# Routing of two tiles at once, and the last layer's experts in order of their token counts

## The chip, the core and the metric

The program runs on one core of one Trainium2 chip. The metric is the device time of one execution in microseconds (us); of several runs the median counts. The engines are PE (matrix multiplication; PEld is its weight load), DVE (VectorE), ACT (ScalarE), POOL (GpSimd) and SP (SyncE, which here issues the DMAs of the weights). The kernel leaves the order within each engine's queue to a planner that simulates a timeline when the program is built; `issue_after` holds instructions of a block behind a given one.

## What is computed

Two layers of a transformer over 256 latent and 256 context tokens with 1024 features. Each layer is a mixer followed by a mixture of experts. What matters here is the second part:

```python
def grouped_moe(h, router_w, router_b, w1, w3, w2):
    ...
    scores = jax.nn.softmax((t @ router_w).astype(jnp.float32), axis=-1)
    sel = scores + router_b.astype(jnp.float32)
    gscore = jnp.sum(lax.top_k(sel.reshape(-1, N_GROUPS, EXPERTS_PER_GROUP), TOP_K)[0], axis=-1)
    best = jnp.argmax(gscore, axis=-1)
    ...
    _, idx = lax.top_k(jnp.where(in_grp, sel, -jnp.inf), TOP_K)
    ...
    for e in range(N_EXPERTS):
        a = jax.nn.silu(t @ w1[e]) * (t @ w3[e])
        y = y + gate[:, e:e + 1] * (a @ w2[e])
    return y.reshape(shape)
```

There are 16 experts in 4 groups, and each token goes to 2 of them. Layer 0 routes 512 tokens (4 tiles of 128), the last layer only the 256 latent tokens (2 tiles), which are 512 assignments. The weights of one expert are six units of 1 MiB: w1 and w3 in four, w2 in two. All values are fp32; matmuls run in fp32 or as split parts in fp32r.

## The kernel before

**Norm and routing.** The last part of the mixer takes the tiles one by one: it adds the residual (L955), squares (L959), transposes (`norm2_turn`, L1102), and multiplies with the router weights (`norm2_logits`, L1115 to L1127). `norm2_rows` makes the normalized rows h2 (L1142, L1144; some halves go through ACT and POOL, L1139 and L1140). `route_tile` turns the logits of one tile into two one-hot choices O and their sum r_ind (L1288) by a chain of small DVE instructions on 16 columns, and into gate weights. `route_slots` counts on PE how many earlier tokens chose the same expert (`earlier`, L1318) and gives each token its slot: r_sg (L1305) in the last layer, one-hots r_oh (L1328) in layer 0. There `dispatch` then makes the index lists, a branch follows for overflowing experts (L1836), and the rows of the first expert are gathered by an indirect DMA. Three buffers for gathered rows are zeroed by POOL (L1458).

**The last layer's experts** (`experts_blocks`). The 16 experts go one after the other in their natural order, 64 slots each. `group` gathers the tokens of four experts by matmuls with one-hots goh (L1583, L1572). The loop at the end of the function goes over the experts: `act` (silu L1631, gate L1635) for e, the branch, the first half of `inner` for e+1 (L1618), `turn` (L1641, L1643) and `outer` for e (L1618 on aT), then the second half of `inner` for e+1. Every second expert the rows of a pair are split in two parts (`parts`, L1698, L1699) and added to the residual in PSUM (`combine`, L1690). The residual itself is put there by eight matmuls with the identity (L1728) at the start of the function.

An expert with more than 64 tokens needs a second pass, `extra`, over the same weights. It stands in a branch for every expert:

```python
            with tc.If(v > B):
                extra(e)
```

The count v is loaded into a register on PE, ACT and DVE; all three go through the branch.

**Weights.** `weights` gives the units in the order of their use, and `prefetch` issues their loads on SP into a ring of 11 units of 1 MiB. A load waits until PE has used what lay in its buffer.

## Time and profile before

| | us |
|---|---|
| median of 3 runs | 1284.99 (1282.62 to 1285.81) |
| profiled execution | 1283.58 |
| its span in the profile | 1281.8 |
| PE busy | 1182.5 (92%) |
| DVE busy | 733.4 (57%) |
| ACT busy | 585.9 (46%) |
| POOL busy | 222.8 (17%) |

The busy times are means over stages that differ: the span has two mixers, two routings and two expert stages. A matmul group of `xN` lists its instructions; an fp32 matmul is two of them. "ACTq" or "PEq" as what ended a wait is the engine's queue itself, here its branch, not an instruction that computes. [...]

### The profile page before, as it was taken

The page shows a single profiled execution, that of the slowest core. Times are in us where ns is not written, and L with a number is a line of the kernel's source. Part 1 is how long each engine was busy: PE and PEld are TensorE (multiplying, and loading weights), DVE is VectorE, ACT ScalarE, POOL GpSimd, SP SyncE. Part 2 cuts the span into 40 slices and gives each one's busy share as a digit, 9 for nine tenths or more (in the row PEclk, how much of TensorE's full clock was granted, in tenths as well). Part 3 has the DMA queues.
Part 4 walks back from the last instruction along what each step waited for, and adds up shares of the span by engine and source line. Part 5 has one row for each costly group of instructions (what it writes and reads, how often), then busy time and mean ns, then how long its engine had stood idle before and what let it go on. Part 6 is the DMA issues. An engine that isn't in the chain of part 4 may idle for free. (4 is left out here: it accounts for less than half of the span.)

```text
span 1281.8 us, 16756 instructions
## 1 busy us (share of the span) xinstructions
PE 1182.5 (92%) x6133; PEld 802.3 (63%) x6133; DVE 733.4 (57%) x1284; ACT 585.9 (46%) x1001; POOL 222.8 (17%) x251
## 2 busy tenths in 40 slices
PE   5899999999987999999999799999997898989885
PEld 3588887546755788887776588986554434334322
DVE  3475454365587999998889957544558222211112
ACT  4374343255333888888776565533443111111011
POOL 2205012022043111111104524003202000000000
PEclk9999999999987999999999999999997999999898
DMA  9524115983437999999976351217966399999951
GB/s 348 217 99 177 66 66 195 352 302 120 149 148 265 362 381 378 380 383 357 354 292 239 117 178 46 99 67 239 369 255 222 145 389 411 418 407 414 379 194 71
DMA packets 55744, 322.05 MB, mean 251 GB/s; under 512 B 9211, under 2 KB 9371, under 8 KB 22360
## 3 DMA queue, kind: packets, MB, share of 16 engines
q1 hardware_dynamic: 48552, 302.77, 61.6%
q0 software_dynamic: 7088, 17.92, 4.4%
q8 instruction: 63, 1.03, 0.3%
q14 instruction: 41, 0.34, 0.1%
HBM read 313.65 MB, written 14.68 MB: 256 GB/s over the span
## 5 line engine op out<-in xcount | busy, mean ns | idle before, releaser
L191 DVE TENSOR_TENSOR wlo<-raw,whi 128x1024 fp32r<-128x1024 f32 x264 | 323.3, 1248 | 81.3 <-ACT whi L190 78.6
L190 ACT CAST whi<-raw 128x1024 fp32r<-128x1024 f32 x264 | 272.6, 1049 | 173.1 <-PE ps L1390 28.6
L1618 PE MATMUL ps<-raw,xT 128*64 128x512 f32 x424 | 111.3, 611 | 19.3 <-ACTq L1743 10.4
L1389 PE MATMUL ps<-whi,xh 128*128 128x512 f32 x256 | 103.0, 403 | 0.7 <-ACT whi L190 0.7
L1391 PE MATMUL ps<-wlo,xh 128*128 128x512 f32 x256 | 99.4, 400 | 4.1 <-DVE wlo L191 4.0
L1390 PE MATMUL ps<-whi,xl 128*128 128x512 f32 x256 | 101.4, 396 | 0.0
L362 PE MATMUL ps<-hl,whi 128*128 128x512 f32 (+1 forms) x256 | 96.5, 378 | 4.8 <-DVE hl L342 4.8
L363 PE MATMUL ps<-hh,wlo 128*128 128x512 f32 (+1 forms) x256 | 94.0, 376 | 4.4 <-DVE wlo L191 4.4
L361 PE MATMUL ps<-hh,whi 128*128 128x512 f32 (+1 forms) x256 | 94.1, 378 | 1.3 <-ACT hh L339 1.2
L1618 PEld LDWEIGHTS ps<-raw,xT 128*64 128x64 f32 x424 | 33.2, 139 | 76.7 <-issue 49.6
L379 PE MATMUL ps<-whi,hh 128*128 128x512 f32 x176 | 71.7, 408 | 0.0
L380 PE MATMUL ps<-whi,hl 128*128 128x512 f32 x176 | 70.0, 398 | 0.0
L381 PE MATMUL ps<-wlo,hh 128*128 128x512 f32 x176 | 68.6, 397 | 0.0
L1635 DVE SCALAR_TENSOR_TENSOR s<-ps,ggate,s 64x512 f32<-64x512 f32 x16 | 12.0, 749 | 92.5 <-ACT s L1631 68.4
L220 PE MATMUL ps<-raw,svec 128*32 128x512 f32 (+1 forms) x416 | 62.1, 606 | 1.9 <-DMA raw<-in_ada_w_dram 1.9
L1654 DVE TENSOR_TENSOR yp<-ps,X 64x512 f32<-64x512 f32 x32 | 22.0, 689 | 70.9 <-PE ps L1618 70.7
L1391 PEld LDWEIGHTS ps<-wlo,xh 128*128 128x128 f32 x256 | 48.0, 188 | 22.1 <-DVE wlo L191 11.4
L362 PEld LDWEIGHTS ps<-hl,whi 128*128 128x128 f32 x256 | 50.5, 197 | 14.1 <-DVE hl L342 5.5
L1618 PE MATMUL ps<-raw,aT 128*64 128x512 f32 x232 | 58.2, 594 | 1.0 <-ACT aT L1643 1.0
L363 PEld LDWEIGHTS ps<-hh,wlo 128*128 128x128 f32 x256 | 49.8, 197 | 12.6 <-DVE wlo L191 4.6
L361 PEld LDWEIGHTS ps<-hh,whi 128*128 128x128 f32 x256 | 49.8, 196 | 10.6 <-ACT hh L339 2.6
L1389 PEld LDWEIGHTS ps<-whi,xh 128*128 128x128 f32 x256 | 48.3, 189 | 11.7 <-ACT whi L190 1.9
(422 smaller groups left out, 2289.1 us busy)
## 6 DMA issues: line engine op xcount, KB each, us to landing
raw<-in_exp_w_dram SPq DMA_DIRECT2D x174, 1024.0 KB, 7.6
raw<-in_ada_w_dram SPq DMA_DIRECT2D x48, 1024.0 KB, 6.9
raw<-in_w_in_dram SPq DMA_DIRECT2D x28, 1024.0 KB, 8.5
raw<-in_w_out_dram SPq DMA_DIRECT2D x8, 1024.0 KB
whi<-in_exp_w_dram SPq DMA_DIRECT2D x16, 512.0 KB, 13.5
wlo<-in_exp_w_dram SPq DMA_DIRECT2D x16, 512.0 KB, 7.7
yd<-oz SPq DMA_DIRECT2D x8, 512.0 KB, 8.8
rpbt<-in_rpb_rows_dram POOLq DMA_DIRECT2D x16, 256.0 KB, 12.3
```

The lines of the kernel that those rows point to most:

```text
L190: self.nc.scalar.copy(hi[:, :n], raw[:, k:k + n])
L191: self.nc.vector.tensor_tensor(lo[:, :n], raw[:, k:k + n], hi[:, :n].bitcast(F32), op=ALU.subtract)
L361: nc.tensor.matmul(o, hi[:, kk, s], self.hh[:, k, tok], start=k == 0, stop=False)
L362: nc.tensor.matmul(o, hi[:, kk, s], self.hl[:, k, tok], start=False, stop=False)
L363: nc.tensor.matmul(o, lo[:, kk, s], self.hh[:, k, tok], start=False, stop=k == KT - 1)
L379: nc.tensor.matmul(acc[g], self.hh[:, k, s], hi[:, kk], start=k == 0, stop=False)
L380: nc.tensor.matmul(acc[g], self.hl[:, k, s], hi[:, kk], start=False, stop=False)
L381: nc.tensor.matmul(acc[g], self.hh[:, k, s], lo[:, kk], start=False, stop=k == KT - 1)
L1389: nc.tensor.matmul(ps, xh, hi[:, kk], start=k == 0, stop=False)
L1390: nc.tensor.matmul(ps, xl, hi[:, kk], start=False, stop=False)
L1391: nc.tensor.matmul(ps, xh, lo[:, kk], start=False, stop=k == KT - 1)
L1618: mm = nc.tensor.matmul(o[c:c + B], x, wt, start=k == 0, stop=k == n - 1, tile_position=(0, c), skip_group_check=True)
```

## The change

`route_tile` becomes `route_tiles`: two tiles go through one chain, with instructions on two tiles' columns wherever no per-token scalar is needed. Layer 0 routes tiles 0 and 1 within the loop over the tiles and tiles 2 and 3 behind it; the last layer routes its two tiles at once behind the last logits. `norm2_rows` loses the form that used ACT and POOL, and the rows of the last two tiles come ahead of the last logits; h2l of the last tile comes behind r_ind (`norm2_parts`). The eight matmuls of the residual move from the start of `experts_blocks` to behind the last logits. The three buffers of layer 0 are zeroed by ACT instead of POOL.

In the last layer `sort` orders the experts 4 to 15 by falling count on DVE, and moves their counts, slots and gates along. Positions 0 to 3 keep their experts. The weights from position 4 on are loaded from an address that SP takes from a register, loaded from `order`. Of 512 assignments at most seven of the sorted twelve can have more than 64, so positions 11 to 15 have no branch. A matmul of the identity into the next accumulator is added before each branch. `extra` transposes its one-hots earlier and uses two PSUM buffers.

```diff
-                    self.route_tile(l, n - 1)
                     self.norm2_rows(l, tiles[n - 1])
+                if n == 2:
+                    self.route_tiles(l, 0)
...
+        self.norm2_rows(l, tiles[-2])
         self.norm2_turn(g, 1)
+        self.norm2_scale(g)
+        self.norm2_rows(l, g, False)
         self.norm2_logits(l, g, 1)
-        self.route_tile(l, n - 1)
-        self.norm2_rows(l, tiles[-2])
-        with self.tc.issue_after(self.scored.ins):
-            for i in range(n):
-                self.route_slots(l, i)
-        self.route_tile(l, n)
-        self.route_slots(l, n)
-        self.norm2_rows(l, tiles[-1])
+        if not l:
+            with self.tc.issue_after(self.scored.ins):
+                self.route_slots(l, 0)
+        if l:
+
+            self.acc = [[self.ps() for _ in range(2)] for _ in tiles]
+            with self.tc.issue_after(self.scored.ins):
+                for i, t in enumerate(tiles):
+                    for h in range(2):
+                        nc.tensor.matmul(self.acc[i][h], self.ident, self.X[:, t, h * 512:(h + 1) * 512], start=True,
+                                         stop=False, skip_group_check=True)
+        self.route_tiles(l, n - 1)
+        self.route_slots(l, n - 1)
+        if l:
+            self.norm2_parts(g)
...
+    def norm2_scale(self, g):
+        q = self.work.tile([P, 4], F32, name="n2q", bufs=4)
+        nc.vector.tensor_scalar(q[:, 0:1], self.ss2[:, 0, g:g + 1], 1.0 / D, EPS, op0=ALU.mult, op1=ALU.add)
+        nc.vector.scalar_tensor_tensor(q[:, 1:2], self.ss2[:, 1, g:g + 1], 1.0 / D, q[:, 0:1], op0=ALU.mult, op1=ALU.add)
+        nc.gpsimd.tensor_tensor(self.r2[:, g:g + 1], q[:, 1:2], self.mhalf[:, 0:1], op=ALU.pow)
+
+    def norm2_rows(self, l, g, parts=True):
...
-            spare = g == 3 and half == 1 or g == 2 and l == 0
-            if spare:
-                nc.scalar.mul(h2[:, s], self.X[:, g, s], self.r2[:, g:g + 1])
-                nc.gpsimd.tensor_tensor(h2[:, s], h2[:, s], self.A2[r][:, s], op=ALU.mult)
-            else:
-                nc.vector.scalar_tensor_tensor(h2[:, s], self.X[:, g, s], self.r2[:, g:g + 1], self.A2[r][:, s],
-                                               op0=ALU.mult, op1=ALU.mult)
-            (nc.vector if half and not spare else nc.gpsimd).tensor_tensor(h2[:, s], h2[:, s], self.S2[r][:, s],
-                                                                           op=ALU.add)
+            nc.vector.scalar_tensor_tensor(h2[:, s], self.X[:, g, s], self.r2[:, g:g + 1], self.A2[r][:, s],
+                                           op0=ALU.mult, op1=ALU.mult)
+            (nc.vector if half or g == 3 else nc.gpsimd).tensor_tensor(h2[:, s], h2[:, s], self.S2[r][:, s], op=ALU.add)
...
+            if parts:
+                self.norm2_parts(g)
         else:
             nc.sync.dma_start(self.hd[i * P:(i + 1) * P], h2)
 
+    def norm2_parts(self, g):
+
+        with self.tc.issue_after(self.chosen.ins) if g == 3 else ExitStack():
+            self.nc.vector.tensor_tensor(self.h2l[:, g - 2], self.h2, self.h2h[:, g - 2].bitcast(F32), op=ALU.subtract)
...
-            for e in range(NE):
+            for p in range(NE):
+                x = p
+                if p >= FIXED:
+                    x = self.nc.values_load(self.order[0:1, p - FIXED:p - FIXED + 1], engines=(ET.SP,), min_val=0,
+                                            max_val=NE - 1)
                 for u in range(6):
-                    yield w[l, e, u]
+                    yield w[l, p, u] if p < FIXED else w[l, ds(x, 1), u].rearrange("o p f -> (o p) f")
...
+    def route_tiles(self, l, i):
...
+        V.tensor_reduce(mx, self.logits[:, w], axis=AX.X, op=ALU.max, negate=True)
+        for j in each:
+            nc.scalar.activation(sc[:, j], self.logits[:, i + j], AF.Exp, bias=mx[:, j:j + 1], accum_out=sm[:, j:j + 1])
         V.reciprocal(rs, sm)
-        V.scalar_tensor_tensor(sel, sc, rs, self.rb, op0=ALU.mult, op1=ALU.add)
...
+        for j in each:
+            V.scalar_tensor_tensor(sel[:, j], sc[:, j], rs[:, j:j + 1], self.rb, op0=ALU.mult, op1=ALU.add)
+
+        s4 = sel.rearrange("p n (g e) -> p (n g) e", g=4)
+        p6 = pr.rearrange("p n g e -> p (n g) e")
+        V.tensor_tensor(p6[:, :, 0:3], s4[:, :, 0:3], s4[:, :, 1:4], op=ALU.add)
...
+        for j in each:
+            V.scalar_tensor_tensor(key[:, j, 0:4], gs[:, j], gm[:, j:j + 1], self.rank16[:, 0:4], op0=ALU.is_equal,
+                                   op1=ALU.mult)
+        V.tensor_reduce(k1, key[:, :, 0:4], axis=AX.X, op=ALU.max)
+        V.tensor_tensor(low, key[:, :, 0:4], wide(k1, 4), op=ALU.is_lt)
+        V.scalar_tensor_tensor(s4, bcast(low.rearrange("p n (g o) -> p (n g) o", o=1), [P, 4 * n, 4]), NEG, s4,
+                               op0=ALU.mult, op1=ALU.add)
+        O = R["O"]
+        for k in range(2):
+            V.tensor_reduce(c0, sel, axis=AX.X, op=ALU.max)
+            for j in each:
+                V.scalar_tensor_tensor(key[:, j], sel[:, j], c0[:, j:j + 1], self.rank16, op0=ALU.is_equal, op1=ALU.mult)
+            V.tensor_reduce(c1, key, axis=AX.X, op=ALU.max)
+            V.tensor_tensor(O[:, w, k], key, wide(c1, NE), op=ALU.is_equal)
+            if k == 0:
+                V.scalar_tensor_tensor(sel, O[:, w, 0], 4 * NEG, sel, op0=ALU.mult, op1=ALU.add)
+        self.chosen = V.tensor_tensor(R["ind"][:, w], O[:, w, 0], O[:, w, 1], op=ALU.add)
...
+        both, wt = t("both", [2, NE]), t("wt", [2])
+        with self.tc.issue_after(self.chosen.ins):
+            for j in each:
+                G.tensor_tensor(both[:, j], O[:, i + j], bcast(sc[:, j, None, :], [P, 2, NE]), op=ALU.mult)
+                nc.scalar.activation(R["gw"][:, i + j], both[:, j], AF.Copy, accum_out=wt[:, j, 0:1])
+            V.reciprocal(wt[:, :, 1], wt[:, :, 0])
+            for j in each:
+                nc.scalar.mul(R["gw"][:, i + j], both[:, j], wt[:, j, 1:2])
+                if l:
+                    G.tensor_tensor(R["gate"][:, i + j], R["gw"][:, i + j, 0], R["gw"][:, i + j, 1], op=ALU.add)
...
+        pp = self.ps()[:, 0:n * NE].rearrange("p (n e) -> p n e", n=n)
+        for j in range(n):
+            self.earlier(i + j, pp[:, j])
+            self.routed = V.scalar_tensor_tensor(R["sg"][:, w], pp, 1.0, R["ind"][:, w], op0=ALU.add, op1=ALU.mult)
...
+            both = self.moeA.tile([P, n, 2, NE], F32, name="rt_both2")
+            for c in range(2):
+                V.tensor_tensor(both[:, :, c], R["O"][:, w, c], pp, op=ALU.mult)
+            V.tensor_reduce(R["slot"][:, w], both, axis=AX.X, op=ALU.add)
+            for j in range(n):
+                self.slotted(i + j)
...
-            nc.gpsimd.memset(x, 0.0)
+            nc.scalar.mul(x.rearrange("p (k s) -> p k s", k=KT), bcast(self.slots[:, None, :], [P, KT, P]), 0.0)
...
+        def sort():
...
+            c = R["cntf"][:, FIXED:]
+            V.scalar_tensor_tensor(key, c, 16.0, self.rank16[:, FIXED:], op0=ALU.mult, op1=ALU.add)
+            V.tensor_tensor(tmp, row(key), col(key), op=ALU.is_gt)
+            V.tensor_reduce(rank, tmp, axis=AX.X, op=ALU.add)
+            V.tensor_tensor(mat, row(rank), col(self.slots[:, 0:NS]), op=ALU.is_equal)
+
+            def moved(dst, src):
+                V.tensor_tensor(tmp, mat, row(src), op=ALU.mult)
+                V.tensor_reduce(dst, tmp, axis=AX.X, op=ALU.add)
+            moved(val, self.rank16[:, FIXED:])
+            V.tensor_scalar(self.order, val, -1.0, 16.0, op0=ALU.mult, op1=ALU.add)
+            moved(val, c)
+            V.tensor_copy(cnts, val)
+            for i in range(nt):
+                moved(sgs[:, i], R["sg"][:, i, FIXED:])
+                moved(gts[:, i], R["gate"][:, i, FIXED:])
...
-            for i in range(nt):
-                for e in range(4):
-                    self.routed = V.tensor_scalar(oh[:, i, :, e], slots1, R["sg"][:, i, 4 * g + e:4 * g + e + 1], None,
-                                                  op0=ALU.is_equal)
+            for b in range(2):
+                for i in range(nt):
+                    V.tensor_tensor(oh[:, i, b], bcast(slots1[:, b, None, :], [P, 4, B]),
+                                    bcast(SG(i, g)[:, :, None], [P, 4, B]), op=ALU.is_equal)
...
-            ps = self.ps()
-            inner(lambda k: x[:, k], W[e], range(KT), ps)
-            aT = turn(*act(ps))
-            ps = self.ps()
...
+            py = self.ps()
+            inner(lambda k: x[:, k], W[e], range(KT), py)
+            aT = turn(*act(py), ps)
...
-        acc = [[self.ps() for _ in halves] for _ in range(nt)]
-        for i in range(nt):
-            for h, s in enumerate(halves):
-                nc.tensor.matmul(acc[i][h], self.ident, X[:, 2 + i, s], start=True, stop=False, skip_group_check=True)
+        acc = self.acc
...
+        sort()
...
+        seven = FIXED + nt * P * 2 // (B + 1)
+
+        def value(e):
+            src = R["cnt"][0:1, 1 + e:2 + e] if e < FIXED else cnts[0:1, e - FIXED:e - FIXED + 1]
+            return nc.values_load(src, engines=(ET.PE, ET.Activation, ET.DVE), min_val=0, max_val=nt * P)
...
-            with tc.If(v > B):
-                extra(e)
+                nc.tensor.matmul(A[e + 1][:, 0:B], self.ident, self.ident[:, 0:B], start=True, stop=True,
+                                 skip_group_check=True)
+            if e < seven:
+                with tc.If(v > B):
+                    extra(e)
             self.prefetch(len(self.raws) - 2)
-            if e + 1 < NE:
+            if e + 1 < seven:
                 v = value(e + 1)
```

## Rows read from the trace of the kernel before

**Rows 1.** Stretches: us; PE, PEld, DVE, ACT, POOL busy (instructions); clock; DMA share; GB/s.
```profile
377.00:403.00 26.00, 14.78 (x95) 9.09 (x96) 21.76 (x101) 8.70 (x24) 11.74 (x16) 0.63 0.82 300
981.00:1002.00 21.00, 13.85 (x73) 8.96 (x73) 16.47 (x74) 5.39 (x16) 9.55 (x15) 0.70 0.27 100
1064.00:1179.00 115.00, 103.53 (x502) 47.69 (x498) 26.18 (x41) 14.25 (x24) 1.31 (x2) 0.99 1.01 412
1190.00:1200.00 10.00, 7.46 (x25) 1.88 (x20) 2.58 (x3) 1.64 (x2) 0.00 (x0) 0.83 1.02 422
1209.00:1234.00 25.00, 21.86 (x96) 10.01 (x94) 3.44 (x5) 1.83 (x4) 0.00 (x0) 0.86 0.70 265
```

**Rows 2.** Timeline of DVE, layer 0 routing: start, length (us), line, output<-input [idle before].
```profile
372.54 0.16 DVE L1263 RECIPROCAL rt_col<-rt_col 128x1 f32<-128x1 f32 x1 [0.47 <-ACT rt_sc L1262]
...
383.09 0.22 DVE L1127 SCALAR_TENSOR_TENSOR logits<-ps,rstd,rbS 128x16 f32<-128x16 f32 x1
...
392.23 0.23 DVE L1284 TENSOR_SCALAR r_o<-rt_key,rt_col 128x16 f32<-128x16 f32 x1
392.50 0.17 DVE L1288 TENSOR_TENSOR r_ind<-r_o 128x16 bf16<-128x16 f32 x1
```

**Rows 3.** Timeline of PE, where the first expert of layer 0 starts.
```profile
402.52 1.73 PE L713 MATMUL ps<-ident,A 128*128 128x128 f32 x7 [5.08 <-PEq L1836]
```

**Rows 4.** Timeline of DVE, routing of the last layer.
```profile
984.26 0.22 DVE L1127 SCALAR_TENSOR_TENSOR logits<-ps,rstd,rbS 128x16 f32<-128x16 f32 x1
...
985.60 1.19 DVE L1277 TENSOR_TENSOR rt_sel<-rt_sel,rt_low 128x16 f32<-128x16 f32 x1
...
994.16 0.18 DVE L1288 TENSOR_TENSOR r_ind<-r_o 128x16 bf16<-128x16 f32 x1
...
1010.71 0.74 DVE L1635 SCALAR_TENSOR_TENSOR s<-ps,ggate,s 64x512 f32<-64x512 f32 x1 [9.32 <-ACT s L1631]
```

**Rows 5.** Timeline of POOL, routing of the last layer.
```profile
984.28 2.48 POOL L1144 TENSOR_TENSOR h<-h,X 128x512 f32<-128x512 f32 x2
```

**Rows 6.** Waits from 1005 us on: who waited <- for whom: us, times, longest.
```profile
PE ps L1618 <- ACTq L1743: 13.8, 9, 2.6
...
PE ps L1618 <- DMA raw<-in_exp_w_dram: 3.9, 4, 1.2
```

**Rows 7.** Timeline of ACT, the last experts: silu (L1631) and the copy ex.
```profile
1179.11 0.59 ACT L1631 ACTIVATE s<-ps 64x512 f32<-64x512 f32 x1 [8.68 <-PE ps L1618]
...
1205.87 0.59 ACT L1631 ACTIVATE s<-ps 64x512 f32<-64x512 f32 x1 [5.21 <-PE ps L1618]
1213.74 0.59 ACT L1664 COPY ex<-ps 128x512 f32<-128x512 f32 x1 [7.28 <-PE ps L1572]
...
1246.08 0.59 ACT L1631 ACTIVATE s<-ps 64x512 f32<-64x512 f32 x1
...
1256.48 0.59 ACT L1631 ACTIVATE s<-ps 64x512 f32<-64x512 f32 x1 [5.20 <-PE ps L1618]
```

**Rows 8.** Timeline of PE, the last experts: where PE stood, and after the extra.
```profile
1179.80 3.65 PE L1618 MATMUL ps<-raw,xT 128*64 128x512 f32 x16 [0.72 <-ACTq L1743]
...
1192.40 1.07 PE L1618 MATMUL ps<-raw,xT 128*64 128x512 f32 x2 [1.54 <-ACTq L1743]
1194.47 5.34 PE L1618 MATMUL ps<-raw,xT 128*64 128x512 f32 x14 [1.00 <-DMA raw<-in_exp_w_dram]
...
1234.16 3.65 PE L1618 MATMUL ps<-raw,xT 128*64 128x512 f32 x16
...
1246.77 3.65 PE L1618 MATMUL ps<-raw,xT 128*64 128x512 f32 x16 [1.54 <-ACTq L1743]
```

**Rows 9.** Groups of instructions by line, 930 us on: count | busy us, mean ns | idle before.
```profile
L1728 PE MATMUL ps<-X,ident 128*128 128x512 f32 x8 | 5.7, 882 | 0.0
...
L1142 DVE SCALAR_TENSOR_TENSOR h<-X,rstd 128x512 f32<-128x512 f32 x3 | 2.2, 749 | 0.9 <-POOL rstd L1122 0.8
```

**Rows 10.** Waits of the queue of SP from 990 us on.
```profile
SPq L182 <- PE ps L1618: 78.6, 10, 18.5
```

More of the change, by code (lines that the diff above doesn't have):

```diff
@@ L37 @@
 NPT = 4
+FIXED = 4
 ET = mybir.EngineType
@@ L1118, in norm2_logits @@
             return
-        q = w.tile([P, 4], F32, name="n2q", bufs=4)
-        nc.vector.tensor_scalar(q[:, 0:1], self.ss2[:, 0, g:g + 1], 1.0 / D, EPS, op0=ALU.mult, op1=ALU.add)
-        nc.vector.scalar_tensor_tensor(q[:, 1:2], self.ss2[:, 1, g:g + 1], 1.0 / D, q[:, 0:1], op0=ALU.mult, op1=ALU.add)
-        nc.gpsimd.tensor_tensor(self.r2[:, g:g + 1], q[:, 1:2], self.mhalf[:, 0:1], op=ALU.pow)
+        if g not in self.scaled:
+            self.norm2_scale(g)
         part = w.tile([P, 512], F32, name="lpart", tag="t2", bufs=T2)[:, :P]
@@ L1289, in route_tile @@
+        self.chosen = V.tensor_tensor(R["ind"][:, w], O[:, w, 0], O[:, w, 1], op=ALU.add)
         if not l:
-            nc.scalar.mul(R["val"][:, i, :, 0], O, self.tokp[:, i:i + 1])
-            nc.scalar.copy(R["val"][:, i, 1, 1], O[:, 1])
+            for j in range(i, i + n):
+                nc.scalar.mul(R["val"][:, j, :, 0], O[:, j], self.tokp[:, j:j + 1])
+                nc.scalar.copy(R["val"][:, j, 1, 1], O[:, j, 1])
         G = nc.gpsimd
-        G.tensor_tensor(both, O, bcast(sc[:, None, :], [P, 2, NE]), op=ALU.mult)
@@ L1315, in earlier @@
+    def earlier(self, i, pp):
         nc, R = self.nc, self.R
[L1316 removed]
         for j in range(i + 1):
[L1318 to L1320 removed]
+            nc.tensor.matmul(pp, self.tri if j == i else self.onesb, R["ind"][:, j], start=j == 0,
+                             stop=j == i, skip_group_check=True)
     def slotted(self, i, rnd=0):
```

96 lines of the change are left out of this document (36 added, 60 removed).

## The prediction

> **What bounds the kernel now.** I read the windows first. They cut out the stretches that the change touches: the routing of the first layer, the routing of the last layer, and the last layer's experts [rows 1]. Between 377 and 403 us PE is busy for 14.8 of 26 us, at a mean granted clock of 0.63, while DVE is busy for 21.8: a chain of small DVE steps stands between the mixer and the first expert. Between 981 and 1002 us it is the same: DVE 16.5 of 21 us, PE 13.9, clock 0.70. In the last layer's experts (1064 to 1179 us) two things run near full: PE is busy for 103.5 of 115 us, and the DMA engines show a share of 1.01 at 412 GB/s.
>
> Then the timelines of the two routings. In layer 0 the last tile's logits start at 383.09 and the last r_ind ends at 392.67, 9.6 us later [rows 2]; the first expert's transposes start at 402.52 [rows 3]. In the last layer the same two points are 984.26 and 994.34, 10.1 us apart [rows 4]. The reader is to see that two tiles' chains take turns there, and that a 16-element step lasts 1.19 us, where others last 0.17 to 0.23, while POOL works on the rows h [rows 2, 4, 5].
>
> Then the waits of the expert stage: before the L1618 matmuls PE stands 13.8 us in 9 waits released by ACT's branch and 3.9 us in 4 waits for weights [rows 6]. Last, the ACT and PE timelines: one silu per expert gives the pace [rows 7]. Only one expert runs `extra`: the only ex copy follows the 14th silu, so it is expert 13. The extra fills the window 1209 to 1234, and the next expert starts at 1234.16 [rows 1, 8]: 25 us. During it the DMA share is 0.70 instead of 1.01.
>
> **The change part by part.** Minus is a gain.
>
> *Layer 0, routing by pairs.* After the last logits one chain of 26 DVE instructions serves two tiles. Six are followed by one that doesn't depend on them; I put 0.1 us on each of those, and 0.22 on each of the other 20, by the dependent steps 392.23 and 392.50, 0.27 apart, whose durations are 0.23 and 0.17 [rows 2]: 5.0 us. The exps come in between: DVE pauses 0.47 us for one [rows 2], so some 0.7 for two. The chain is 5.7 us against 9.6: -3.9. Back come four one-hots instead of two behind the last r_ind and a wider multiplication, some +0.6. The rows of tiles 2 and 3 now take seven half-row steps on DVE, each about 0.7 us by the nearest row [rows 9], 5 us between the last X and its logits; PE and ACT work for the logits meanwhile, but a logits instruction can land behind two of them: 0 to +1.7, I take +0.9. Sum -2.4. Bounds: 0, if it is not the chain but the gather's landing or the branch at L1836 that sets 402.52 [rows 3] and these don't move along, and -4. I take -2.4 since gather and dispatch stand behind r_ind in program order. The three zero fills that go from POOL to ACT are activations of 1024 elements, about 1 us each; ACT is busy for 8.7 of the 26 us [rows 1], so 0.
>
> *Last layer, routing.* The chain is 5.7 against 10.1: -4.4. The rows of the last tile are four DVE steps of about 0.7 us [rows 9] ahead of the logits: 0 to +1.7, taken +0.8. ACT's cast h2h of 1024 elements, about 1 us, may come before the exps: 0 to +1, taken +0.4. POOL no longer works on these rows, so the 1.19 us step and its like [rows 4] should shrink; that is within the -4.4. The residual's eight matmuls (5.7 us, 0.88 each at the low clock [rows 9]) move ahead of r_ind. Their place today puts r_sg some 0.6 us late; against that stands the h2l subtraction, now behind r_ind: 0 together. But PE then idles up to 2 us before the gather, and in this stretch the clock did fall after idling (0.70 on the mean [rows 1]): the gather's 32 instructions of 256 columns are about 3.7 us, by half of the 0.23 us that one of 512 takes (16 in 3.65 [rows 8]), and double at half clock: 0 to +3.7, taken +0.7. Sum -2.5, bounds -4.5 and +1.5.
>
> *Sort.* 18 small DVE instructions of at most 144 elements; 512 elements take 0.75 us and 16 take 0.17 to 0.23 [rows 2, 9], so some 0.3 each, 5 to 6 us. DVE waits 9.32 us at exactly that place, while PE runs the first expert [rows 4]: 0. Without that cover the whole 6 us would stand before the first act.
>
> *Expert order and register addresses.* Expert 13 holds the largest count from the fifth on, so its extra moves from the 14th to the 5th place and still costs 25 us. SP loads twelve registers, each at the head of six weight DMAs. What is queued behind such a load is the weight stream; who waits is PE, but only once the units in flight are used up. The ring holds 11 units of 1 MiB, 6 of them in use, so 5 are in flight: 5 x 2.55 us (1 MiB at 412 GB/s) = 12.7 us of cover. No row shows a register load on SP; nearest is the wait of PE at a branch, 0.72 to 1.54 us at four late experts [rows 8]. I take 0; bounds 0 and 12 x 1.54 = +18.5, which needs the cover to be gone at each one.
>
> *No branch for the last five.* At experts 11, 12 and 14 PE stands 0.72, 1.54 and 1.54 us, released by ACT's branch [rows 8]; I add 0.7 for the 14th place (no row, as the extra ran there) and 0.3 for the last: -4.8. At expert 12 the branch wait and the weight wait of 1.00 that follows it are where the clock fell: 0.83 in 1190 to 1200 us [rows 1], that is a third of the time at half speed, 1.7 us of matmuls: -1.7. Bounds: -8, and 0 if PE waits for the same ACT and DVE work at a semaphore.
>
> [...]
>
> *What is late next: the weights.* In 1064 to 1179 a position's six units take 6 x 2.55 = 15.3 us. The last four steps of silu (expert 11 to 15) took 26.8 (two of them), 40.2 and 10.4 us [rows 7]. Without the extra's 25, the waits named above and the clock, these are 46 us of work. Four positions' weights are 4 x 15.3 = 61.1 us. Five units are ahead when they begin, because the extra at the 5th place lets the ring fill and the experts up to the 11th, with their gathers, are no faster than the weights: 61.1 - 12.7 = 48.4, so 2.4 us of new waits for weights: +2.4. Bounds: 0, and +15 if no lead is left. In the before, the extra itself covered this place. Of the four older weight waits (3.9 us [rows 6]) the one at expert 12 goes, as the ring is fuller: -1.0 (0 to -3.9).
>
> *The added matmul* on the identity before each branch: two instructions of 64 columns, well under the 0.23 us of one with 512 [rows 8], with their weight loads 0.25 us for both. Where a branch follows PE waits anyway; on the rest +1.0 (0 to +3.8 for fifteen).
>
> Sum: -2.4 - 2.5 - 4.8 - 1.7 + 2.4 - 1.0 + 1.0 = -9.0 us. The profiled execution took 1283.58 us, so 1274.6; the median of the runs, 1284.99, lies 1.4 higher, so I predict 1276.
>
> **The rivals.** *More than that.* The weights keep up to the end (no +2.4), both routings give what their chains say (-3.9 and -4.4), the clock stays up: about -15, 1270. For it: 412 GB/s is a mean, and the DMA engines have slack in the extra. Against: a wait for weights, 1.00 us, stood at expert 12 already.
>
> *Waits that only move.* PE meets ACT at a semaphore instead of the branch, or the weights take all of 6.5 back; layer 0's start is set by the gather; what is left is the last layer's routing: -2.5, 1282.5. For it: PE's waits name ACT, which is busy with the cast gyh or the silu just then, not with the branch. Against: the silu has 3.65 us of matmuls of the next expert [rows 8] to hide behind once the branch is gone.
>
> *The weights become the bound: slower.* Place: positions 11 to 15. If the lead is gone when they begin, four steps last 61.1 us instead of 52.4 (the four of today less 25): +8.7. With the routings' -4.9 and the added matmuls' +1.0 that is +4.8, 1290. It decides once fewer than two of the five units are ahead: each unit is worth 2.55 us, and with none ahead 15 us of the work's shortfall is bare. For it: the DMA share is 1.01 already, and the extra now leaves the DMA engines idle in mid stream, for about 25 - 12.7 = 12 us, not at the end. Against: those 12 us are PE's too, and the ring is full after them.
>
> [...]
>
> *The change doesn't do what it says:* the register loads on SP hold the stream. At 18.5 us, less the gains of 9: 1294. It decides from 12.7 us for one load, or from a ring that is never full. Against: in the expert stage SP waits 78.6 us in ten waits for PE to free a buffer [rows 10].
>
> **How the numbers follow.** Forecast 0.58 (1270 to 1281 by itself), more than that 0.12, waits that only move 0.17, weights bound 0.09, register loads 0.04. About 0.3% (3.9 us) is what a measurement can tell from no change. Faster 0.58 + 0.12 = 0.70, same 0.17, slower 0.13. The range 1268 to 1286 leaves out half of the first rival and the slower ones.
>
> **What would show it.** The last r_ind 3 to 4 us nearer to the logits in both layers, and no 16-element step over 0.6 us in the last layer's; the first expert about 2.5 us earlier than the layer's start suggests; one ex copy after the 5th silu; no branch after the 11th position, and PE's waits for weights there of 1 to 5 us in sum; sort wholly within DVE's idle time. The prediction is wrong if waits for weights after the 11th position exceed 8 us, if SP stands at a register load while PE waits for weights, or if the first expert of either layer starts no earlier.

## The result, and the profile after

The changed kernel takes 1294.07 us (median of 4 runs, 1292.67 to 1298.14); the kernel before took 1283.80 beside it (1281.86 to 1285.81). The ratio is 1.0089, 95% interval 1.0064 to 1.0114: 0.9% or some 10 to 11 us slower. The prediction was 1276 us, faster. The profiled execution took 1292.67 us, its span is 1290.9 (1281.8 before).

The windows first, with the columns of [rows 1]; the clock is the one granted to PE, which stands at 1.00 or 0.50 in the traces of both kernels:

```profile
377.00:403.00 26.00, 15.36 (x95) 9.78 (x96) 19.43 (x87) 10.89 (x32) 5.20 (x9) 0.60 0.83 313
981.00:1002.00 21.00, 13.77 (x66) 9.45 (x67) 16.85 (x62) 4.80 (x16) 4.58 (x8) 0.76 0.33 123
1003.00:1018.00 15.00, 15.00 (x66) 4.91 (x66) 2.65 (x8) 3.54 (x5) 1.35 (x2) 1.00 0.00 1
1018.00:1080.00 62.00, 54.63 (x256) 22.58 (x255) 13.94 (x21) 7.50 (x13) 1.21 (x2) 0.97 0.98 388
1080.00:1115.00 35.00, 31.49 (x148) 14.82 (x149) 4.13 (x6) 2.29 (x5) 0.00 (x0) 0.95 0.47 187
1115.00:1260.00 145.00, 136.64 (x626) 55.55 (x624) 29.77 (x42) 18.07 (x31) 1.21 (x2) 0.99 0.99 397
```

Read the last two columns from the third line on. Between 1003 and 1018 us the DMA engines carry next to nothing (a share of 0.00, 1 GB/s), while PE is busy throughout (15.00 of 15 us): the ring of weights is full, and no buffer comes free. From 1018 to 1260 the share is near 1, but for 35 us around the extra (0.47), which now stands at the fifth place. PE is nearly as full (136.64 of 145 us in the last window): weights and PE run side by side.

The routings, on DVE (start, length, line; as [rows 2, 4]); layer 0 first, then the last layer:

```profile
380.85 0.23 DVE L1137 SCALAR_TENSOR_TENSOR logits<-ps,rstd,rbS 128x16 f32<-128x16 f32 x1
...
382.86 0.18 DVE L1286 TENSOR_REDUCE rt_col<-logits 128x2 f32<-128x32 f32 x1
...
389.65 0.19 DVE L1317 TENSOR_TENSOR r_ind<-r_o 128x32 bf16<-128x32 f32 x1
```

```profile
986.57 0.23 DVE L1137 SCALAR_TENSOR_TENSOR logits<-ps,rstd,rbS 128x16 f32<-128x16 f32 x1
...
993.21 0.19 DVE L1317 TENSOR_TENSOR r_ind<-r_o 128x32 bf16<-128x32 f32 x1
993.32 1.22 DVE L1169 TENSOR_TENSOR h2l<-h,h2h 128x1024 fp32r<-128x1024 f32 x1
994.45 0.18 DVE L1343 SCALAR_TENSOR_TENSOR r_sg<-ps,r_ind 128x32 f32<-128x32 f32 x1
...
995.32 1.46 DVE L1652 TENSOR_TENSOR goh<-slots,r_sg 128x256 fp32r<-128x256 f32 x4
```

In the last layer logits and last r_ind are 6.83 us apart (end of r_ind; 10.1 before), but h2l and all the one-hots goh now follow r_ind. In layer 0 the distance is 9.0 us (9.6 before): the second pair's chain begins 2.0 us after its logits, since the first pair's was still running.

PE at the first expert of the last layer:

```profile
1002.91 7.09 PE L1687 MATMUL ps<-raw,xT 128*64 128x512 f32 x32
...
1010.58 0.43 PE L1812 MATMUL ps<-ident 128*128 128x64 f32 x2
1010.95 4.08 PE L1687 MATMUL ps<-raw,xT 128*64 128x512 f32 x17
...
1018.33 0.43 PE L1710 MATMUL ps<-ident,s 64*128 64x64 f32 x4 [0.30 <-PEq L1815]
...
1022.56 5.35 PE L1687 MATMUL ps<-raw,aT 128*64 128x512 f32 x16 [2.80 <-issue]
```

L1812 is the added identity matmul. Behind it stand thirty of the 32 matmuls of expert 1's first product, and only then comes branch 0 (PEq L1815). In the kernel before, the branch stood ahead of expert 1's matmuls. The first weight load on SP's queue once the ring has been filled, before and then after:

```profile
1010.24 16.21 SPq L182 DMA_DIRECT2D raw<-in_exp_w_dram  x9
```

```profile
1018.15 17.03 SPq L183 DMA_DIRECT2D raw<-in_exp_w_dram  x9
```

From the first expert's first matmul that is 8.6 us before (it began at 1001.61) and 15.2 after. The extra could read expert 0's first four units again, so their buffers are free only when PE has passed branch 0. SP's queue shows it; between 1003 and 1019 us its wait is for PE's branch:

```profile
SPq L183 <- PEq L1815: 11.3, 1, 11.3
```

The waits of PE from 1005 us on (as [rows 6]); no wait for ACT's branch is left, but more for weights, and 2.8 us behind six register loads on PE's queue (0.30 to 0.31 us each, one every 0.69 to 0.79 us; with their register operations from 1018.35 to 1022.50 us):

```profile
PE ps L1687 <- DMA raw<-in_exp_w_dram: 10.5, 8, 2.3
PE ps L1687 <- issue: 2.8, 1, 2.8
```

ACT at the fullest expert: silu, the copy ex, the extra's silu (as [rows 7]):

```profile
1070.65 0.59 ACT L1700 ACTIVATE s<-ps 64x512 f32<-64x512 f32 x1 [4.14 <-PE ps L1687]
1083.72 0.58 ACT L1733 COPY ex<-ps 128x512 f32<-128x512 f32 x1 [7.14 <-PE ps L1641]
1093.62 0.59 ACT L1700 ACTIVATE s<-ps 64x512 f32<-64x512 f32 x1 [8.38 <-PE ps L1687]
```

The extra comes after the fifth silu, as planned, but 13.1 us behind it.

Theory 1 after this reading: the added matmuls are the loss, as they let the next expert's matmuls go ahead of the branch. Rivals: the extra's new place (2), the register loads and the sort (3, 6), the routing (4), and the added matmuls' own time (5). Each kernel below was timed beside the kernel before; ratios are to it, with 95% intervals.

### The profile page after: what moved, and what is told of

Same layout as the page of the kernel before. It is cut to its first block, busy times and chain, and to the rows that moved or that the text cites. A ratio compares the mean times of both kernels' runs of the same rounds, so it can differ in the third digit from the quotient of the medians.

```text
span 1290.9 us, 16866 instructions
## 1 busy us (share of the span) xinstructions
PE 1199.9 (93%) x6163; PEld 808.3 (63%) x6163; DVE 728.4 (56%) x1236; ACT 587.3 (45%) x1006; POOL 205.9 (16%) x233
## 5 line engine op out<-in xcount | busy, mean ns | idle before, releaser
L1687 PE MATMUL ps<-raw,xT 128*64 128x512 f32 x424 | 116.7, 603 | 11.2 <-DMA raw<-in_exp_w_dram 10.5
L1687 PE MATMUL ps<-raw,aT 128*64 128x512 f32 x232 | 63.2, 612 | 3.8 <-issue 2.8
L1430 PEld LDWEIGHTS ps<-wlo,xh 128*128 128x128 f32 x256 | 48.0, 188 | 23.6 <-DVE wlo L192 13.1
L1700 ACT ACTIVATE s<-ps 64x512 f32<-64x512 f32 x17 | 10.0, 591 | 109.2 <-PE ps L1687 109.2
```

Of the source, the lines that this page charges most:

```text
L1430: nc.tensor.matmul(ps, xh, lo[:, kk], start=False, stop=k == KT - 1)
L1687: mm = nc.tensor.matmul(o[c:c + B], x, wt, start=k == 0, stop=k == n - 1, tile_position=(0, c), skip_group_check=True)
```

## Experiments

**No added matmul at expert 0.**

```
-                nc.tensor.matmul(A[e + 1][:, 0:B], self.ident, self.ident[:, 0:B], ...)
+                if e:
+                    nc.tensor.matmul(A[e + 1][:, 0:B], self.ident, self.ident[:, 0:B], ...)
```

> The changed kernel without the added identity matmul ahead of the first branch alone; the other fourteen stay. PE's order at expert 0 is then that of the kernel before: the branch, then the next expert's matmuls. Theory 1 (late start of the weight stream: the ring's first units come free only once PE has passed branch 0, which the added matmul puts behind 15 matmuls of expert 1): the first weight load of SP after the ring is filled goes from 1018.2 to 1010-1012 us, and the time falls by 6 to 8 us, to 1286-1288. Rival 2 (the extra of the fullest expert at the 5th place leaves the DMA engines idle in mid stream): the first load comes earlier too, but the ring is then full before the extra all the same; 1292-1295. Rival 3 (register loads on PE and SP): 1292-1295.

Measured: 1.0042 (1.0021 to 1.0064), 1289.71 us: 0.47% or 6 us below the changed kernel by the ratios, 4.4 us by the medians (expected: 1286 to 1288). The first load (SP's queue) is back, 8.6 us after the first expert's start:

```profile
1008.74 18.51 SPq L183 DMA_DIRECT2D raw<-in_exp_w_dram  x9
```

The first load is theory 1's, and the ratio's fall is at the low end of its 6 to 8 us. The traces show less. ACT at the fifteenth expert's silu, in the changed kernel and then here:

```profile
1247.57 0.59 ACT L1700 ACTIVATE s<-ps 64x512 f32<-64x512 f32 x1 [3.17 <-PE ps L1687]
```

```profile
1241.84 0.59 ACT L1700 ACTIVATE s<-ps 64x512 f32<-64x512 f32 x1 [3.17 <-PE ps L1687]
```

Counted from the first expert's start (1002.91 and 1000.10) these are 244.7 and 241.7 us: of the 6.6 us by which the stream starts sooner, 2.9 are left by then. That fits rival 2's account, by which the ring is full before the extra all the same. At the end none is left, 288.5 us against 288.0; behind that silu e1 ran at a lower granted clock (0.72 from 1250.1 to 1255.1 us; the last sixteen matmuls on aT took 5.35 us instead of 3.65). So the first load's cause is shown; that branch 0 is half of the loss rests on the ratio alone.

**No added matmul at all.**

```
-                nc.tensor.matmul(A[e + 1][:, 0:B], self.ident, self.ident[:, 0:B], ...)
```

> The changed kernel without any of the fifteen added identity matmuls, all else as changed. Theory 1: the start of the stream is back at 1010-1012 us (-6 to -8), but on the other positions PE stands at the branches again before the next expert's matmuls (0 to +5, hidden where the weights are what is waited for): 1286-1291. Rival 2: 1292-1297, since the place of the extra is unchanged. Rival 3: 1292-1297.

Measured: 0.9992 (0.9971 to 1.0014), 1280.25 us. The fifteen matmuls are the whole loss: 0.97%, 12.5 us. In the traces 10.9 us of it lie between the first expert and the end (288.0 and 277.1 us). The six or seven us beyond e1 were not in my account of theory 1. ACT shows where they may be, since the extra now follows its silu by 3.7 us, not 13.1:

```profile
1064.01 0.59 ACT L1700 ACTIVATE s<-ps 64x512 f32<-64x512 f32 x1 [0.94 <-PE ps L1687]
1067.68 0.59 ACT L1733 COPY ex<-ps 128x512 f32<-128x512 f32 x1 [3.08 <-PE ps L1641]
```

**Natural order.** Without sort and registers, a branch at all sixteen.

```
-        four = lambda nat, moved: lambda i, g: (moved[...] if g else nat[:, i, 0:4])
+        four = lambda nat, moved: lambda i, g: nat[:, i, 4 * g:4 * g + 4]
-        sort()
-        seven = FIXED + nt * P * 2 // (B + 1)
+        seven = NE
...
-                if p >= FIXED:
+                if False:
```

> The changed kernel with the experts in their own order: no sort, no register addresses, a branch at all sixteen positions; the routing by pairs, the added matmuls and the rewritten extra stay. The only extra stands at the 14th place again. Theory 1: the late start of the stream stays (+6 to +8 against the kernel before) and the waits at branches stay away: 1286-1292. Rival 2 (extra at the 5th place): the whole loss and more is gone: 1278-1284. Rival 3 (registers): 1280-1285. Rival 4 (routing): 1292-1295.

**Natural order by register.** As above, but the sort runs and moves nothing.

```
-            V.scalar_tensor_tensor(key, c, 16.0, self.rank16[:, FIXED:], op0=ALU.mult, op1=ALU.add)
+            V.tensor_copy(key, self.rank16[:, FIXED:])
-        seven = FIXED + nt * P * 2 // (B + 1)
+        seven = NE
```

> As the kernel in natural order, but the sort runs (on a key that leaves the order as it is), and the weights of experts 4 to 15 are loaded by a register's address, and the counts, slots and gates are the sorted copies. Against the kernel in natural order it adds only the sort and the register loads. Theory 1 and rival 2: within 2 us of it. Rival 3 (registers and sort): 5 to 10 us slower than it, near the changed kernel's 1294.

Measured: 1.0032 (1.0013 to 1.0050) and 1.0039 (1.0021 to 1.0057). With the matmuls in, the natural order takes back 0.57% by the ratios and not all of the loss; sort and registers are worth 0.07% here, within the intervals nothing. But in the traces the natural order gains nothing behind the first expert: from there to the end it is 289.0 and 288.9 us, and 288.0 in the changed kernel. The first expert of layer 0, ahead of all that differs, starts at 397.06 and 400.39 us instead of 401.56. So a part of the 0.57%, and of e1's 0.47%, may be the changed kernel's four runs; that was not settled.

**The kernel before with the added matmuls alone** (and the extra's new wording, which saves the PSUM bank that they claim).

```
             if e + 1 < NE:
                 A[e + 1] = self.ps()
+                nc.tensor.matmul(A[e + 1][:, 0:B], self.ident, self.ident[:, 0:B], ...)
             with tc.If(v > B):
```

> The kernel before with one part of the change alone: the identity matmul ahead of each branch (and the extra in its new wording, which needs one PSUM bank less and which the matmul requires). Routing, order, branches as before. Theory 1, widened by the runs so far (the matmuls are the loss: they let the next expert's matmuls stand ahead of the branch, so the ring's buffers come free later): the first weight load some 6 us later after the first expert's start, the stretch from the first expert to the end 287 to 290 us instead of 280, the time 6 to 10 us above before. Rival 2 (the loss needs the extra at the 5th place): within 3 us of before.

Measured: 1.0030 (1.0008 to 1.0052), 4 us above before: a loss, but half of what I expected, and the interval takes in rival 2's 3 us. The first load comes as late as theory 1 says, 15.2 us after the first expert's start (1002.30):

```profile
1017.54 17.82 SPq L182 DMA_DIRECT2D raw<-in_exp_w_dram  x9
```

So 6.6 us lost at the start became 3.4 from the first expert to the end (283.6 instead of 280.2 us). In the kernel before, the stream pauses once more behind its start (a DMA share of 0.50 from 1020 to 1025 us, 2.5 us lost); here it doesn't (1.01).

**The routing, with the residual's new place and the rewritten extra, without the rest.** The edits of the natural order (e3), and:

```
-                nc.tensor.matmul(A[e + 1][:, 0:B], self.ident, self.ident[:, 0:B], ...)
```

> The changed kernel's routing by pairs, moved residual and rewritten extra alone: natural order, sixteen branches, no sort, no registers, no added matmuls. Theory 1: what the routings are worth and no more: 1 to 4 us below before, with the stretch from the first expert to the end as before, 279 to 281 us. Rival 4 (the routing loses): 1 us or more above before.

Measured: 0.9943 (0.9921 to 0.9966), 1275.46 us: 7.3 us below before. This version beats both kernels. But from the first expert to the end it takes 274.7 us, 5.5 less than before, and the routing lies ahead of that. Two places show in PE's timelines, each first in the kernel before and then here. The 32 first-product matmuls of the extra:

```profile
1214.38 9.26 PE L1618 MATMUL ps<-raw,ex 128*64 128x512 f32 x32 [0.68 <-ACT ex L1664]
```

```profile
1210.38 7.09 PE L1687 MATMUL ps<-raw,ex 128*64 128x512 f32 x32
```

The same work took 2.2 us less, as the granted clock was 1.00 in 1206 to 1226 us here and 0.87 in 1206 to 1232 before. And the matmuls of expert 1 behind branch 0:

```profile
1011.87 3.65 PE L1618 MATMUL ps<-raw,xT 128*64 128x512 f32 x16 [2.52 <-ACTq L1743]
```

```profile
1008.07 3.65 PE L1687 MATMUL ps<-raw,xT 128*64 128x512 f32 x16 [1.06 <-PEq L1812]
```

Before, they came 1.5 us later after the first expert's start, behind ACT's branch. But these 1.5 us are not kept: ACT's silus of the 14th and 15th expert here,

```profile
1205.65 0.59 ACT L1700 ACTIVATE s<-ps 64x512 f32<-64x512 f32 x1 [8.70 <-PE ps L1687]
...
1235.60 0.59 ACT L1700 ACTIVATE s<-ps 64x512 f32<-64x512 f32 x1 [3.17 <-PE ps L1687]
```

come 206.4 and 236.3 us after the first expert; before it was 204.3 and 244.5 [rows 7]. The gain lies between the two, where the extra runs: 29.95 us instead of 40.21. The clock is 2.2 of these 10.3. The extra was rewritten here, and no run tells the routing from that; in e5, with the rewritten extra, the old routing and the added matmuls, it is 40.7 us.

**Falling order, all sixteen branches, no matmuls.** As e2, and:

```
-        seven = FIXED + nt * P * 2 // (B + 1)
+        seven = NE
```

> The kernel by falling number of tokens without the added matmuls, as e2, but with a branch at all sixteen positions instead of the first eleven. Its only difference from e2 is the five branches. The prediction's sum says 4.8 us above e2. Theory 1 (the weight stream sets the end, waits at branches only turn into waits for weights): within 2 us of e2.

Measured: 0.9994 (0.9972 to 1.0016) against 0.9992 for the same with eleven branches. The five branches are worth nothing that these runs can measure. The waits of PE from 1005 us on show why (sixteen branches):

```profile
PE ps L1687 <- DMA raw<-in_exp_w_dram: 13.7, 9, 3.3
PE ps L1687 <- PEq L1813: 2.3, 5, 1.1
```

PE's waits for ACT's branch are gone here with all branches in place, and from 1180 us on, where the five stand, PE waits 9.1 us for weights and 0.3 at a branch.

**Each branch ahead of its own expert's matmuls.**

```
+        def maybe(e):
+            if e >= seven:
+                return
+            W[e] = self.take(6)
+            v = value(e)
+            with tc.If(v > B):
+                extra(e)
+        maybe(0)
         A[0] = self.ps()
         first(0, range(KT))
...
-            if e < seven:
-                with tc.If(v > B):
-                    extra(e)
...
+                maybe(e + 1)
```

> As e2 (falling order, no added matmuls), but each expert's branch stands ahead of its own matmuls instead of behind them: branch 0 before the first expert's matmuls, branch e+1 where branch e was. A buffer of the ring then comes free as soon as the expert's own matmuls have read it. Theory 1: the first weight load after the ring is filled comes 5 to 6 us sooner after the first expert's start than in e2 (3 us instead of 8.6), and the time is 3 to 6 us below e2. Rival (PE, not the stream, sets the end): within 1 us of e2, with longer idle times of the DMA engines instead.

Measured: 1.0000 (0.9975 to 1.0025), as e2. The first load comes 3.7 us after the first expert's start, as expected, but that start itself is 2 us later (1002.48), as the branch's wait (1.56 us) and the matmuls of `mod5`, which the edit moves too, now stand ahead of it. The DMA engines pause ahead of the extra as well (a share of 0.50 from 1045 to 1055 us). From the first expert to the end it is 275.2 us, 1.9 less than e2, for a stream that starts 5 us sooner. My estimate of 3 to 6 us was wrong; the rival held.

**No added matmul at places 0 and 4.**

```
+                if e not in (0, FIXED):
                     nc.tensor.matmul(A[e + 1][:, 0:B], self.ident, self.ident[:, 0:B], ...)
```

> The changed kernel without two of the fifteen added matmuls: ahead of branch 0 (as e1) and ahead of the branch of position 4, the one whose extra runs. Theory 1: the extra then starts 4 us after its expert's silu, as in e2, and not 12, so the first of the two holes in the DMA stream goes; 4 to 7 us below e1's ratio of 1.0042, that is 0.999 to 1.001. Rival 5 (the fifteen matmuls cost by their own time on PE, 0.39 us each, and by their wait): within 1.5 us of e1.

Measured: 0.9996 (0.9972 to 1.0019). The matmul at place 4, the one whose extra runs, costs 0.46%, and the other thirteen nothing that is measurable. The extra's ex comes 7.1 us after its silu (12.3 in e1), not 4 as I wrote. The windows around the extra and behind it, in e1 and then here:

```profile
1075.00:1110.00 35.00, 31.49 (x124) 12.89 (x124) 4.12 (x6) 2.29 (x5) 0.00 (x0) 0.85 0.41 157
1110.00:1257.00 147.00, 139.29 (x629) 56.51 (x628) 29.77 (x42) 18.09 (x31) 1.21 (x2) 0.98 0.99 400
```

```profile
1075.00:1110.00 35.00, 32.11 (x146) 12.97 (x144) 4.88 (x7) 2.52 (x5) 0.00 (x0) 0.98 0.43 171
1110.00:1250.00 140.00, 132.89 (x612) 53.84 (x610) 28.92 (x41) 17.01 (x29) 1.21 (x2) 1.00 1.01 415
```

The hole itself is hardly shorter (0.43 against 0.41 busy); the stream is back at full pace earlier behind it (415 against 400 GB/s) and ends 7 us sooner. Here the traces agree with the ratio. The fifteenth silu comes 234.0 us after the first expert (241.7 in e1):

```profile
1234.75 0.59 ACT L1700 ACTIVATE s<-ps 64x512 f32<-64x512 f32 x1 [3.23 <-PE ps L1687]
```

Of these 7.7 us the clock is 2.2: the extra's two products took 9.41 and 5.19 us in e1, and 8.79 and 3.65 here.

**The added matmuls behind the branch.** The same fifteen, after the If.

```
                 with tc.If(v > B):
                     extra(e)
+            if e + 1 < NE:
+                nc.tensor.matmul(A[e + 1][:, 0:B], self.ident, self.ident[:, 0:B], ...)
```

> The changed kernel with all fifteen added matmuls, but each behind its branch instead of ahead of it. The same work on PE; only what may stand ahead of the branch differs. Theory 1 (what costs is that the branch, and with it the release of the ring's buffers, comes later): the same as e2 without the matmuls, ratio 0.998 to 1.002. Rival 5 (own time on PE): 5 us above e2, about 1.004.

Measured: 1.0007 (0.9982 to 1.0033), against 1.0089 ahead of it. Same work, other place, and the extra's ex is back at 3.7 us behind its silu: what costs is what stands ahead of the branch, as theory 1 says, and rival 5 is out as the main cause. A smaller cost of their own is not excluded: in the trace the stretch from the first expert to the end is 281.3 us, 4.2 more than in e2, while the ratios differ by 0.15%, within the intervals.

**The fullest at the 15th place.**

```
-            V.scalar_tensor_tensor(key, c, 16.0, self.rank16[:, FIXED:], ...)
+            V.scalar_tensor_tensor(key, c, -16.0, self.rank16[:, FIXED:], ...)
+            V.tensor_scalar(key[:, NS - 1:NS], self.rank16[:, NE - 1:NE], -65536.0, None, op0=ALU.mult)
```

> As e7 (order by register, no added matmuls, sixteen branches), but experts 4 to 14 by rising number of tokens and expert 15 last, so that the fullest stands at the 15th place. When its extra runs, the last expert's weights are all but loaded, and the hole in the stream can't delay anything. Theory 2 (the place of the extra decides whether its hole in the stream counts): the DMA share stays near 1.0 to the end of the stream at about 228 us after the first expert's start (249 to 250 in e6 and e7); the stretch from the first expert to the end is 270 to 273 us instead of 277.5 (e7) and 274.7 (e6); ratio 0.991 to 0.995. Rival 6 (registers and order themselves cost, not the place): as e7, 0.999.

Measured: 0.9995 (0.9973 to 1.0017): as e7, where I expected 0.991 to 0.995. The stream behaves as forecast, in windows:

```profile
1012.00:1225.00 213.00, 194.93 (x940) 82.63 (x940) 45.77 (x66) 25.96 (x46) 2.42 (x4) 0.99 1.00 406
...
1225.00:1258.00 33.00, 29.64 (x120) 11.13 (x122) 3.43 (x5) 2.20 (x5) 0.00 (x0) 0.92 0.23 90
```

It has no hole and ends about 230 us after the first expert's start (1003.49). But PE then has the extra, the last expert and nothing to overlap them with:

```profile
1217.21 0.59 ACT L1701 ACTIVATE s<-ps 64x512 f32<-64x512 f32 x1 [3.17 <-PE ps L1688]
1224.91 0.58 ACT L1734 COPY ex<-ps 128x512 f32<-128x512 f32 x1 [1.77 <-PE ps L1642]
...
1258.97 0.59 ACT L1701 ACTIVATE s<-ps 64x512 f32<-64x512 f32 x1 [8.69 <-PE ps L1688]
```

41.8 us lie between the last two experts' silus. The hole in the stream was exchanged for a tail of PE: removing one bound uncovered the other.

**No extra, in falling and in natural order** (e7 and e6 with this edit; the tokens beyond 64 of the fullest expert are left out).

```
-                with tc.If(v > B):
+                with tc.If(v > 4 * B):
```

> As e7, but the branch compares with 256 instead of 64 tokens, so no extra is run: the tokens of the fullest expert beyond 64 are left out of the result. Theory 1 and 2: without the extra there is no hole; the stream ends about 226 us after the first expert's start and the stretch to the end is 253 to 256 us, 22 to 24 us less than e7: an extra at the 5th place costs its whole length of some 23 us. If the weights, not PE, cover a part of it, the fall is 17 us or less, the length of the hole alone.

> As e6, but the branch compares with 256 instead of 64 tokens, so no extra is run (the tokens of the fullest expert beyond 64 are left out of the result). Theory 2: as e12, 1257 to 1259 us, so that the extra costs 17 us at the 14th place and 22 at the 5th. Rival 6: 4 to 6 us below e12, 1252 to 1254 us, so that the extra costs the same 22 us at either place.

Measured: 0.9814 (0.9780 to 0.9847) and 0.9786 (0.9756 to 0.9815): 1258.11 and 1255.09 us. The extra costs 21.6 us of median at the fifth place and 20.4 at the 14th: nearly the same (23.1 and 20.1 by the ratios, 19.9 and 22.6 in the traces from the first expert on). The second time lies between the two forecasts. The stream alone, in the windows of the two:

```profile
1008.00:1227.00 219.00, 202.06 (x942) 83.55 (x944) 46.18 (x67) 26.69 (x47) 2.41 (x4) 0.98 1.00 407
```

```profile
1007.00:1225.00 218.00, 200.33 (x950) 82.91 (x952) 46.09 (x67) 26.50 (x47) 2.41 (x4) 0.99 1.00 409
```

218 to 219 us at a share of 1.00 and 407 to 409 GB/s: from the first release of a buffer on I take that as a floor under the stage, an estimate from these two windows. PE is busy for 92% of it.

**Natural order by register, no matmuls.** The edits of e4, and:

```
-                nc.tensor.matmul(A[e + 1][:, 0:B], self.ident, self.ident[:, 0:B], ...)
```

> As e6 (natural order, sixteen branches, no added matmuls), but the sort runs on a key that keeps the order, and experts 4 to 15 come by register address and sorted copies. Against e7 only the order differs, against e6 only sort and registers. Theory 2 (the place of the extra, 14th against 5th, is what e7 loses to e6): as e6, ratio 0.994 to 0.996, stretch from the first expert to the end 274 to 276 us. Rival 6 (sort and register loads cost it): as e7, ratio 0.998 to 1.001, stretch 277 to 279 us.

Measured: 0.9977 (0.9955 to 1.0000), between the two theories: 0.34% above e6, 0.17% below e7. Together with e12 and e14 (0.28% apart without any extra) it puts some 3 to 4 us on sort and registers and 2 or less on the place. Each of these differences is about as large as its uncertainty; how the 0.5% between e6 and e7 divides stays open. From the first expert to the end e13 and e7 take the same 277.5 us.

## Why the prediction was wrong

One chain of kernels adds the change up: routing, residual and rewritten extra 0.9943; order, sort and registers 0.9994; five branches gone 0.9992; added matmuls 1.0089. My terms beside it:

- **The added matmuls: +1.0 forecast, +12.5 us measured (e2). This step failed.** I priced their work on PE ("0 to +3.8 for fifteen"). In this group of the changed kernel, by line and form, thirty instructions take 5.9 us, 0.39 for each of the fifteen, where I had put 0.25:

```profile
L1812 PE MATMUL ps<-ident 128*128 128x64 f32 x30 | 5.9, 279 | 0.0
```

  but behind the branch they cost nothing that is sure (e10). Ahead of it, the next expert's matmuls follow them past the branch: thirty instructions at branch 0. The added matmul claims the PSUM bank before the branch; that this is why the planner lets the others pass was not shown. Who waits for the branch? SP, for the buffers that the extra may still read. That question, which I asked of every added wait, I didn't ask of an added instruction that lets others pass. I had read SP's queue [rows 10], but only the first line of that view; the second is SP's wait for PE's branch in the kernel before:

```profile
SPq L182 <- PEq L1743: 57.9, 12, 12.8
```

  Two places count. At the branch whose extra runs, the extra starts some 9 us later and the stream recovers late: 6 us by the ratio, 7.7 by the traces (e9). At branch 0 the full ring stands idle until 1018: 6 us by the ratio, 2.9 by the traces (e1). With the natural order the matmuls cost 0.89% too (e3 against e6; 289.0 and 274.7 us from the first expert to the end), though only 0.3% in the kernel before (e5). Of that 2.5 us are the pause at 1020, which the kernel before has of itself; the rest was not located.
- **The bound.** "Two things run near full" was right, and the weights were named as a rival, at positions 11 to 15 and with a chance of 0.09. The stream presses on the whole stage: it needs 218 us without an extra. But a later start or a hole did not come out at the end as it was, for PE is nearly as full (92% of these 218 us). A start 6.6 us late cost 3.4 in e5; one 5 us sooner gave 1.9 in e8; closing the hole gave nothing (e11).
- **Five branches and the clock, -6.5 forecast: 0 measured** (e2 against e7: 0.02%, with an uncertainty of 0.3%). The waits for ACT's branch did go, all 13.8 us of [rows 6], but they are gone with all sixteen branches too (e7), and PE waits for weights instead: 10.5 us in the changed kernel and 13.7 in e7 against 3.9. That is the second rival's "the weights take all of 6.5 back". What took ACT's part away was not separated. The bound that I gave, 0, was the answer, though not by the condition that I put on it.
- **New weight waits +2.4, old ones -1.0:** the sign was right, the account was not. Behind the twelfth silu the changed kernel's PE waits 4.1 us for weights, within the 1 to 5 that I named as a sign, but from 1005 us on it is 10.5. The extra at the fifth place does leave a hole, as the rival said; yet the place matters little. An extra costs 20 to 23 us at either place (e12, e14), and at the 15th place a PE tail takes over (e11).
- **Sort 0, registers 0:** the sort is hidden in DVE's idle time, as forecast (DVE still idles 5.59 us before the first act). SP's twelve register loads ran one behind the other from 1000.06 to 1006.52 us, 0.26 to 0.28 us each, ahead of the first load at 1018.15 and while PE was busy for all 6.46 us; that SP stands at one while PE waits was not seen. The e12 to e14 pair leaves up to some 4 us for both. That the rival of the register loads gave 1294, the measured time, is chance: it needed 18.5 us from them.
- **Layer 0, -2.4 forecast.** From the point where both kernels copy h2T (364.50 and 364.98 us) to the first expert (402.52 and 401.56), 1.4 us are gained. The chain shrank by 0.6 only, not 3.9, since two chains now follow each other on DVE; the logits come 2.7 us sooner. Of these 3.3 us, 1.9 are given back behind r_ind (9.85 us to the first expert before, 11.72 after), where I had put 0.6.
- **Last layer, -2.5 forecast: -0.3.** From the last X to the first expert it is 21.76 us before and 21.44 after. The chain gave 3.3 of the 4.4 forecast, but 2.2 are taken back behind r_ind and 0.7 by the rows ahead of the logits. Of the 2.2, h2l and the one-hots are 1.1, which I had put at 0; the other 1.2 are the gather, which took 5.65 us at a granted clock of 0.70 and 4.49 us at 1.00 before, where I had put 0.7. PE stood idle for 2.15 us before it, as forecast.

The routings themselves come to -1.8 in the two traces, where -4.9 was forecast. That e6 gains 7.3 is for the most part the expert stage of e6, as told there: the extra and what follows it, 2.2 us of it by the clock, the rest without a shown cause.

## What to carry to other kernels

Ask of every instruction moved ahead of a branch or a wait what is released behind that point: here the buffers that the branch's body could still read were held until PE had passed it, and SP waited 11.3 us for that at branch 0. When a stage's DMA share is 1.0 all along, look at what a change does to the start of that stream and to the holes in it before counting removed waits on the engines: here they turned into waits for weights (13.8 us at ACT's branch before and none in e7; 3.9 us for weights before and 13.7 in e7). But price the start and the holes only as far as the engine beside them has room: PE is busy for 92% of the stream (e12, e14), a start 5 us sooner gave 1.9 us (e8), and closing the hole gave nothing (e11). An added instruction should be looked up in the order that comes out, since here one added matmul let thirty matmul instructions pass ahead of a branch.

## What the runs showed that I had not expected

The same stretch of unchanged code ran at another granted clock in the two profiled executions. The windows 748 to 754 us, before and after:

```profile
748.00:754.00 6.00, 4.66 (x20) 3.57 (x21) 6.00 (x11) 3.06 (x7) 4.28 (x4) 1.00 0.53 210
```

```profile
748.00:754.00 6.00, 4.66 (x13) 3.47 (x14) 6.00 (x11) 3.04 (x7) 4.27 (x4) 0.72 0.62 233
```

PE has the same busy time and the same idle wait (1.34 us) there, but the granted clock is 1.00 in one and 0.72 in the other; seven matmuls fewer fit in, and 1.6 us of delay remain behind it. Across the profiles the first expert of layer 0 starts between 396.8 and 402.7 us, more than the routing was worth; how much of that is such shifts was not added up. Two single traces are therefore compared from a common event, not from the span's start, and differences under 0.3% only by repeated runs (the 95% intervals of the ratios reach 0.18 to 0.34% to each side).

Six register loads on PE between two matmuls stand in an idle stretch of 2.80 us, and the sixteen matmuls behind it ran in 5.35 us, where sixteen take 3.60 elsewhere; the granted clock was 0.66 there (1022.9 to 1027.9 us).
